# Paged values of a hybrid decoder step: eight pages and the new values of a sequence in one run of products, nine page buffers

## The chip, the cores and the metric

The kernel runs on one core of one Trainium2 chip. The metric is the device time of one execution in microseconds (us), the median of several runs. The engines are named as in the profile: PE (TensorE, with PEld for its weight loads), DVE (VectorE), ACT (ScalarE), POOL (GpSimd) and SP (SyncE, which here issues nearly all DMAs).

## The reference, cut to what matters

The program is one step of a decoder layer: a prompt of 16 + 1024 tokens, and eight sample sequences of four new tokens each, whose past keys and values lie in pages of 128 tokens. The part that the change touches is the last two lines of the sample attention:

```python
def sb_sample(q, k_new, v_new, k_past, v_past, bias):
    P, T = k_past.shape[1], q.shape[1]
    z = jnp.concatenate([sb_logits(q, k_past, bias), sb_logits(q, k_new, bias)], axis=-1)
    mask = jnp.arange(P + T)[None, :] < (P + jnp.arange(T))[:, None]
    a = stick_break_weights(z, mask)
    return (jnp.einsum('bhqk,bkhd->bqhd', a[..., :P].astype(v_past.dtype), v_past)
            + jnp.einsum('bhqk,bkhd->bqhd', a[..., P:].astype(v_new.dtype), v_new))
```

For each of 8 sequences, `v_past` is 8 pages of 128 tokens by 8 heads by 128 values in fp32 (512 KB a page), picked by a page table.

## The kernel before

The kernel is one Python program whose stages are woven together. Large projections (`inproj`, lines 336 to 353) are products of 128 x 128 weights with up to 402 columns of activations, each as three products of split numbers (lines 347 to 349). A gate (`gate_group`) is one such projection: 8 steps of 18 products, 144 in all, in four weight chunks (`wr_g` loaded by SP, `wh_g` cast by ACT, `wl_g` subtracted by DVE; two buffers of each). After each 6 products it calls `W.beat()`, so a gate has 24 beats. Side work is written as Python generators which a `Weaver` resumes at a beat; `yield 3` means "go on three beats later". What is written in this order is then placed by a scheduler, which fixes for each engine, before the run, one list of instructions. Each engine executes its list strictly in that order and waits on semaphores for its operands.

During gates 5 to 13 the paged values run as such side work:

- `chain(b)` (lines 1274 to 1297) makes the attention weights of sequence b: it loads logits `dz`, takes a softplus (`ds`, by DVE and ACT), running sums (`dc`), four products into `C` (lines 1290 to 1293), adds (lines 1294 and 1295) and an exponential into `As[b]` (`dA`, line 1297).
- `paged_values` (lines 1299 to 1336) loads pages into tiles `vr` (eight buffers) through `page_dma`, and multiplies them (`times_values`, line 1249). A page makes two products, of 32 weight columns with 512 value columns each, into 32 rows of `dO`: an even page into rows 0 to 63, an odd one into rows 64 to 127. Four products of 256 columns with the new values `vn` close a sequence (line 1332); ACT copies `dO` to `osb`, and `sample_out` transposes that into `oT`.
- The pages come in fours. While four are being multiplied, the next four are asked for, one each three beats. The first are asked for after `As[0]` exists and five more beats.

I call an **episode** a stretch in which PE runs products with 32 weight columns with no product of a gate in between. Before, a sequence has two: pages 0 to 3, and pages 4 to 7 with the new values.

Of the kernel before, what the change touches and what calls it, by code (L numbers as in the profile page):

```python
# [10 lines left out]
F32 = mybir.dt.float32  # L11
# [9 lines left out]
P = 128  # L21
# [4 lines left out]
NB = 8  # L26
# [5 lines left out]
HEADS = 8  # L32
GH = 4
DV = 256
NPG = 8
# [54 lines left out]
def hybrid_step(ctx: ExitStack, tc: tile.TileContext, x_prompt, x_sample, cache_k, cache_v, state_gla,  # L90
# [4 lines left out]
    mm = nc.tensor.matmul  # L95
    vec, act, pool = nc.vector, nc.scalar, nc.gpsimd
# [17 lines left out]
    W = Weaver()  # L114
# [80 lines left out]
    with tc.tile_pool(name="xp", bufs=2) as xp, tc.tile_pool(name="xps", bufs=5, space=PSUM) as xps:  # L195
# [109 lines left out]
        for c, (lo, hi) in enumerate(XCHUNKS):  # L305
            n = hi - lo
# [110 lines left out]
    def page_dma(dst, cache, b, i, hs):  # L417

        def load():
            return nc.sync.value_load(pt[:1, b * NPG + i:b * NPG + i + 1], min_val=0, max_val=NPOOL - 1)  # L420
        done = paged.setdefault(cache.tensor.name, [])
        if len(done) < 4:
            pg = load()
        else:
            with tc.issue_after(done[-4]):
                pg = load()
        d = nc.sync.dma_start(dst, cache[0, bass.ds(pg, 1), :, hs, :].rearrange("o p h d -> p (o h d)"))
        done.append(d.ins)
# [109 lines left out]
    with tc.tile_pool(name="sp", bufs=1) as sp, tc.tile_pool(name="sps", bufs=1, space=PSUM) as sps:  # L538
# [64 lines left out]

        def attend_tile(h, qi, qlo, qhi, j, q, kt, V, carry, O):
            nm = f"{h}_{qi}_{j}"
# [63 lines left out]
            if j == jmax:  # L669
                O[qi] = sps.tile([P, 512], F32, tag="O", name=f"O{h}_{qi}")  # L670
            if both:
                o = sps.tile([P, 512], F32, tag="O", name=f"Ob{h}")[:, :n]
                mm(o, V[0][:, j, :], ah[:, :n], start=True, stop=False, skip_group_check=True)
                mm(o, V[0][:, j, :], al[:, :n], start=False, stop=False, skip_group_check=True)
                mm(o, V[1][:, j, :], ah[:, :n], start=False, stop=True, skip_group_check=True)
                O[2] = sp.tile([P, 64], F32, tag="ob", name=f"ob{h}")
                act.copy(O[2][:], o)
                return
            o = O[qi]
            mm(o[:, col:], V[0][:nk, j, :], ah[:nk, :n], start=(j == jmax), stop=False, skip_group_check=True)  # L680
# [116 lines left out]
    with tc.tile_pool(name="gp", bufs=1) as gp, tc.tile_pool(name="gps", bufs=1, space=PSUM) as gps:  # L797
# [330 lines left out]
        for g in range(GH):  # L1128
# [26 lines left out]
            for f in range(2):  # L1155
                v = xtile(f"gv{g}_{f}")
                raws = {}
# [28 lines left out]
    with tc.tile_pool(name="dp", bufs=2) as dp, tc.tile_pool(name="dps", bufs=1, space=PSUM) as dps:  # L1186
# [15 lines left out]
        def softplus_(X, z):  # L1202
            vec.tensor_scalar(X, z, 30.0, None, ALU.min)
            act.activation(X, X, AF.Exp)
            act.activation(X, X, AF.Ln, bias=1.0)
            vec.tensor_tensor(X, z, X, ALU.max)

        def split_(src, shape, rows, tag, nm, bufs=1):
            a = dp.tile(shape, F32R, tag=tag + "h", bufs=bufs, name=f"{nm}_h")
            b = dp.tile(shape, F32R, tag=tag + "l", bufs=bufs, name=f"{nm}_l")  # L1210
            act.copy(a[:rows], src)
            vec.tensor_tensor(b[:rows], src, a[:rows].bitcast(F32), ALU.subtract)
            return a, b
# [31 lines left out]
        def times_values(O, a, v, page):  # L1245

            for f in range(2):
                j = 2 * (page % 2) + f
                mm(O[32 * j:32 * j + 32], a, v[:, f * 512:(f + 1) * 512], start=page < 2, stop=False, skip_group_check=True)

        an = dp.tile([P, NB, 32], F32, tag="an", bufs=1, name="an")
        vn = dp.tile([P, 1024], F32, tag="vn", bufs=1, name="vn")
# [19 lines left out]
        As = {}  # L1272

        def chain(b):

            while b not in z_done:
                yield 2
            z = dp.tile([P, 32, NPG], F32, tag="dz", bufs=1, name=f"dz{b}")
            nc.sync.dma_start(z[:].rearrange("p a r -> p (a r)"), zd[b][:])
            yield 6  # L1280
            vec.tensor_tensor(z[:], z[:], bias32[:].rearrange("p h t -> p (h t)").unsqueeze(2).to_broadcast([P, 32, NPG]), ALU.add)
            s = dp.tile([P, 32, NPG], F32, tag="ds", bufs=1, name=f"ds{b}")
            softplus_(s[:], z[:])
            sh, sl = split_(s[:].rearrange("p a r -> p r a"), [P, NPG, 32], P, "ds", f"ds{b}")
            sf = s[:].rearrange("p a r -> p (a r)")
            vec.tensor_tensor_scan(sf, sm8[:], sf, 0.0, ALU.mult, ALU.add)
            ch, cl = split_(s[:].rearrange("p a r -> p r a"), [P, NPG, 32], P, "dc", f"dc{b}")
            yield 8
            C = dps.tile([P, 256], F32, tag="C", name=f"C{b}")
            mm(C[:], ntri[:], sh[:].rearrange("p r a -> p (r a)"), start=True, stop=False)  # L1290
            mm(C[:], ntri[:], sl[:].rearrange("p r a -> p (r a)"), start=False, stop=False)
            mm(C[:, 32:], nones[:], ch[:, :NPG - 1].rearrange("p r a -> p (r a)"), start=False, stop=False)
            mm(C[:, 32:], nones[:], cl[:, :NPG - 1].rearrange("p r a -> p (r a)"), start=False, stop=True)
            vec.tensor_tensor(z[:], z[:], cn[:, b, :].unsqueeze(2).to_broadcast([P, 32, NPG]), ALU.add)
            vec.tensor_tensor(z[:], z[:], C[:].rearrange("p (r a) -> p a r", r=NPG), ALU.add)
            A = As[b] = dp.tile([P, NPG, 32], F32, tag="dA", bufs=2, name=f"dA{b}")
            act.activation(A[:], z[:].rearrange("p a r -> p r a"), AF.Exp)

        def paged_values():
            W.spawn(chain(0))  # L1300
            while 0 not in As:
                yield 1
            yield 5
            O = None
            pages = [(b, i) for b in range(NB) for i in range(NPG)]
            raws = {}

            def fetch(n):
                if n < len(pages):
                    b, i = pages[n]  # L1310
                    raws[n] = dp.tile([P, 1024], F32, tag="vr", bufs=8, name=f"vr{b}_{i}")
                    page_dma(raws[n][:], cache_v, b, i, slice(0, HEADS))
            for n in range(4):
                fetch(n)
            for n in range(0, len(pages), 4):
                b, i = pages[n]
                while b not in As:
                    yield 1
                if i == 0:
                    if b + 1 < NB:  # L1320
                        W.spawn(chain(b + 1))
                    O = dps.tile([P, 512], F32, tag="O", bufs=2, name=f"dO{b}")
                for e in range(4):
                    fetch(n + 4 + e)
                    yield 3
                for e in range(4):
                    times_values(O, As[b][:, NPG - 1 - i - e, :], raws.pop(n + e), i + e)
                if i == NPG - 4:

                    for j in range(4):  # L1330
                        cs = slice(j // 2 * 256, j // 2 * 256 + 256)
                        mm(O[32 * j:32 * j + 32, cs], an[:, b, :], vn[:, j % 2 * 512 + cs.start:j % 2 * 512 + cs.stop],
                           start=False, stop=True, skip_group_check=True)
                    osb = dp.tile([P, 512], F32, tag="osb", bufs=2, name=f"osb{b}")
                    act.copy(osb[:], O[:])
                    W.spawn(sample_out(b, osb), 4)

        def sample_out(b, osb):

            ps = dps.tile([P, 512], F32, tag="oT", name=f"oT{b}")  # L1340
            for h in range(4):
                nc.tensor.transpose(ps[:, h * P:(h + 1) * P], osb[:, h * P:(h + 1) * P], ident[:])
            a = ps[:]
            for f in range(2):
                own = bass.AP(tensor=a.tensor, offset=a.offset + 48 * f, ap=[list(a.ap[0]), [P + NT, 4], [1, NT], [64, 2]])
                vec.tensor_reduce(osmp[:, 4 * f:4 * f + 4, b * NT:(b + 1) * NT], own, mybir.AxisListType.X, ALU.add)
            return
            yield

        W.spawn(new_keys())  # L1350
        W.spawn(paged_values(), 8)
        for g in range(5, 14):
            gate_group(g)
# [7 lines left out]
    with ExitStack() as out:  # L1361
# [369 lines left out]
        for pair in ((1, 2), (6,), (5, 3), (7, 4)):  # L1731
            for q in range(2):
                banks = [bank(f"b{pair[0]}{q}_{t}") for t in range(4)]
                for p in pair:
                    b = {2: q, 3: 2 + q, 7: 2 + q, 4: q}.get(p)
# [45 lines left out]
```

## Time and profile before

| what | value |
|---|---|
| median of 3 runs | 2034.35 us (2033.86 to 2036.96) |
| the profiled execution | 2034.71 us, its span 2033.0 us |
| PE busy | 2004.2 us, 99% of the span |
| DVE, ACT, POOL busy | 1496.9, 1018.4, 96.1 us |
| granted PE clock, mean | 0.999 |
| stretch with value products | 1438.4 to 1649.4 us |

Busy time of PE is from modelled ends of pipelined matmuls, so that 99% does not mean that each moment carries useful work: the step from one start to the next tells more than a duration. Idle time of another engine costs nothing unless PE waits for it.

### The profile page before, as it was taken

The page shows a single profiled execution, that of the slowest core. Times are in us where ns is not written, and L with a number is a line of the kernel's source. Part 1 is how long each engine was busy: PE and PEld are TensorE (multiplying, and loading weights), DVE is VectorE, ACT ScalarE, POOL GpSimd, SP SyncE. Part 2 cuts the span into 40 slices and gives each one's busy share as a digit, 9 for nine tenths or more (in the row PEclk, how much of TensorE's full clock was granted, in tenths as well). Part 3 has the DMA queues.
Part 4 walks back from the last instruction along what each step waited for, and adds up shares of the span by engine and source line. Part 5 has one row for each costly group of instructions (what it writes and reads, how often), then busy time and mean ns, then how long its engine had stood idle before and what let it go on. Part 6 is the DMA issues. An engine that isn't in the chain of part 4 may idle for free.

```text
span 2033.0 us, 41746 instructions
## 1 busy us (share of the span) xinstructions
PE 2004.2 (99%) x12379; PEld 1852.4 (91%) x12379; DVE 1496.9 (74%) x6163; ACT 1018.4 (50%) x2377; POOL 96.1 (5%) x355
## 2 busy tenths in 40 slices
PE   6999999999999999999999999999999999999998
PEld 5999999999999999999999999999988898788776
DVE  7368888888888888899898888978444338365466
ACT  7356767675766757433535335254433335343342
POOL 0111110101000010000000000000000000000000
PEclk9999999999999999999999999999999999999999
DMA  6345554545555442433342434335767656352485
GB/s 205 98 136 161 143 163 132 175 129 157 151 161 151 141 125 77 142 101 89 103 108 80 126 79 120 90 93 176 243 220 234 221 186 221 104 176 94 141 281 204
DMA packets 371980, 301.92 MB, mean 149 GB/s; under 512 B 42336, under 2 KB 312264, under 8 KB 371752
## 3 DMA queue, kind: packets, MB, share of 16 engines
q1 hardware_dynamic: 371448, 298.73, 49.1%
q8 instruction: 97, 1.59, 0.3%
q14 instruction: 131, 1.07, 0.2%
q10 hardware_dynamic: 304, 0.53, 0.1%
HBM read 241.84 MB, written 57.31 MB: 147 GB/s over the span
## 4 chain that ended last, share of the span: by engine, by line
PE 91%; DVE 3%; DMA 2%; ACT 2%; issue 1%; SPq 0%; DVEq 0%; POOL 0%; POOLq 0%; ACTq 0%
PE acc_g L347 6%; PE acc_g L348 5%; PE acc_g L349 5%; PE b L1682 4%; PE b L1683 4%; PE b L1684 4%; PE acc_gv L347 3%; PE acc_gv L348 3%; PE acc_gv L349 3%; PE acc_k L347 3%; PE acc_k L349 3%; PE acc_k L348 3%; PE acc_q L348 3%; PE acc_q L347 3%; PE acc_q L349 3%; PE acc_v L347 3%
## 5 line engine op out<-in xcount | busy, mean ns | idle before, releaser
L470 DVE SCALAR_TENSOR_TENSOR jk<-kp,qb 128x128 f32<-128x128 f32 x2048 | 593.6, 290 | 46.2 <-DMA qb<-qsd 3.0
L347 PE MATMUL acc_g<-hT,wh_g 128*128 128x368 f32 (+2 forms) x768 | 250.7, 326 | 0.0
L348 PE MATMUL acc_g<-hT,wh_g 128*128 128x368 f32 (+2 forms) x768 | 247.2, 322 | 0.0
L349 PE MATMUL acc_g<-hT,wl_g 128*128 128x368 f32 (+2 forms) x768 | 246.9, 321 | 0.0
L470 DVE DVE_READ_ACCUMULATOR jk<-kp,qb 128x1 f32 x2048 | 167.3, 82 | 0.0
L1682 PE MATMUL b<-ring,f 128*128 128x512 f32 x416 | 163.9, 394 | 1.5 <-DVE y L1547 1.1
L1683 PE MATMUL b<-ring,f 128*128 128x512 f32 x416 | 162.3, 390 | 0.0
L1684 PE MATMUL b<-ring,f 128*128 128x512 f32 x416 | 161.9, 389 | 0.0
L347 PEld LDWEIGHTS acc_g<-hT,wh_g 128*128 128x128 f32 x768 | 144.3, 188 | 12.0 <-issue 10.7
L348 PEld LDWEIGHTS acc_g<-hT,wh_g 128*128 128x128 f32 x768 | 144.4, 188 | 0.7
L349 PEld LDWEIGHTS acc_g<-hT,wl_g 128*128 128x128 f32 x768 | 144.2, 188 | 0.0
L1481 DVE TENSOR_TENSOR ring<-wr,ring 128x512 fp32r<-128x512 f32 x104 | 71.2, 689 | 97.7 <-ACT ring L1480 97.1
L1480 ACT CAST ring<-wr 128x512 fp32r<-128x512 f32 x104 | 64.0, 620 | 134.7 <-PE b L1684 78.1
L347 PE MATMUL acc_gv<-hT,wh_gv 128*128 128x402 f32 (+2 forms) x384 | 130.1, 339 | 0.0
L347 PE MATMUL acc_k<-hT,wh_k 128*128 128x384 f32 (+1 forms) x384 | 126.1, 328 | 0.0
L348 PE MATMUL acc_gv<-hT,wh_gv 128*128 128x402 f32 (+2 forms) x384 | 125.3, 326 | 0.0
L349 PE MATMUL acc_gv<-hT,wl_gv 128*128 128x402 f32 (+2 forms) x384 | 125.0, 326 | 0.0
L349 PE MATMUL acc_k<-hT,wl_k 128*128 128x384 f32 (+1 forms) x384 | 124.7, 325 | 0.0
L348 PE MATMUL acc_k<-hT,wh_k 128*128 128x384 f32 (+1 forms) x384 | 124.4, 324 | 0.0
L347 PE MATMUL acc_q<-hT,wh_q 128*128 128x368 f32 (+2 forms) x384 | 124.3, 324 | 0.0
L348 PE MATMUL acc_q<-hT,wh_q 128*128 128x368 f32 (+2 forms) x384 | 123.6, 322 | 0.0
L349 PE MATMUL acc_q<-hT,wl_q 128*128 128x368 f32 (+2 forms) x384 | 123.3, 321 | 0.0
(483 smaller groups left out, 5263.6 us busy)
## 6 DMA issues: line engine op xcount, KB each, us to landing
kp<-in_cache_k_dram SPq DMA_DIRECT2D x512, 64.0 KB
vr<-in_cache_v_dram SPq DMA_DIRECT2D x64, 512.0 KB
qb<-qsd SPq DMA_DIRECT2D x64, 256.0 KB
wr_g<-in_w_in_dram SPq DMA_DIRECT2D x64, 256.0 KB
wr<-td SPq DMA_DIRECT2D x56, 256.0 KB
tf<-in_w_out_dram SPq DMA_DIRECT2D x48, 256.0 KB
td<-tf SPq DMA_DIRECT2D x48, 256.0 KB
wr<-in_w_out_dram SPq DMA_DIRECT2D x48, 256.0 KB
```

Of the source, the lines that this page charges most:

```text
L347: mm(acc[c][:, :n], wh, hh[k][:, lo:hi], start=(k == 0), stop=False)
L348: mm(acc[c][:, :n], wh, hl[k][:, lo:hi], start=False, stop=False)
L349: W.mark = mm(acc[c][:, :n], wl, hh[k][:, lo:hi], start=False, stop=(k == NK - 1)).ins
L470: ins = vec.scalar_tensor_tensor(jk[:], kp[:], 1.0, qbs[h, b][:, t, :], ALU.mult, ALU.mult, accum_out=zt[:, t, NPG - 1 - i:NPG - i])
L1480: act.copy(wh, r)
L1481: vec.tensor_tensor(wl, r, wh.bitcast(F32), ALU.subtract)
L1682: mm(bk[:], ah, wh, start=first and k == 0, stop=False, skip_group_check=True)
L1683: mm(bk[:], ah, wl, start=False, stop=False, skip_group_check=True)
L1684: W.mark = mm(bk[:], al, wh, start=False, stop=last and k == 7, skip_group_check=True).ins
```

## The change

`paged_values` is written anew. A sequence's eight pages and its new values are multiplied without a `yield` in between. The pages of sequence 0 are asked for at once, one each two beats, before `As[0]` exists. The pages of the next sequence are asked for after the products of this one, 3, 3, 3, 3, 3, 2, 2 and 5 beats apart, so that the last is asked for five beats ahead of the products. There are nine `vr` buffers instead of eight.

```diff
         def paged_values():
             W.spawn(chain(0))
-            while 0 not in As:
-                yield 1
-            yield 5
-            O = None
-            pages = [(b, i) for b in range(NB) for i in range(NPG)]
             raws = {}
 
-            def fetch(n):
-                if n < len(pages):
-                    b, i = pages[n]
-                    raws[n] = dp.tile([P, 1024], F32, tag="vr", bufs=8, name=f"vr{b}_{i}")
-                    page_dma(raws[n][:], cache_v, b, i, slice(0, HEADS))
-            for n in range(4):
-                fetch(n)
-            for n in range(0, len(pages), 4):
-                b, i = pages[n]
+            def fetch(b, i):
+                raws[i] = dp.tile([P, 1024], F32, tag="vr", bufs=9, name=f"vr{b}_{i}")
+                page_dma(raws[i][:], cache_v, b, i, slice(0, HEADS))
+
+            for i in range(NPG):
+                fetch(0, i)
+                yield 2
+            for b in range(NB):
                 while b not in As:
                     yield 1
-                if i == 0:
-                    if b + 1 < NB:
-                        W.spawn(chain(b + 1))
-                    O = dps.tile([P, 512], F32, tag="O", bufs=2, name=f"dO{b}")
-                for e in range(4):
-                    fetch(n + 4 + e)
-                    yield 3
-                for e in range(4):
-                    times_values(O, As[b][:, NPG - 1 - i - e, :], raws.pop(n + e), i + e)
-                if i == NPG - 4:
+                if b + 1 < NB:
+                    W.spawn(chain(b + 1))
+                O = dps.tile([P, 512], F32, tag="O", bufs=2, name=f"dO{b}")
+                for i in range(NPG):
+                    times_values(O, As[b][:, NPG - 1 - i, :], raws.pop(i), i)
 ...
+                if b + 1 < NB:
+                    for i in range(NPG):
+                        fetch(b + 1, i)
+                        yield (3, 3, 3, 3, 3, 2, 2, 5)[i]
```

What is left out are the lines of the new values, `osb` and `sample_out`, which stand one level further left and are the same.

**Place A: the list of SP as the values begin.** `dz0` are the logits of sequence 0, `vr0_0` is its page 0, `wr_g6_1` a weight chunk of gate 6. Before:

```order
L1220 DMA znall_25494<-znd_124 32x256
L1279 DMA dz0_25586<-zd0_84 128x256
L427 ISA
L427 DMA vr0_0_25795<-in_cache_v_dram 128x1024
L185 DMA wr_g6_1_25882<-in_w_in_dram 128x4x128
L1255 DMA vn_25518<-out_6_dram 32x1024
L427 ISA
L427 DMA vr0_1_25806<-in_cache_v_dram 128x1024
```

And now:

```order
L1220 DMA znall_25494<-znd_124 32x256
L427 ISA
L427 DMA vr0_0_25586<-in_cache_v_dram 128x1024
L185 DMA wr_g6_1_25981<-in_w_in_dram 128x4x128
L1255 DMA vn_25518<-out_6_dram 32x1024
L1279 DMA dz0_25597<-zd0_84 128x256
L427 ISA
L427 DMA vr0_1_25611<-in_cache_v_dram 128x1024
```

The load of `dz0` has moved behind page 0, a weight chunk and the new values.

On DVE, the list of the same place, from the first use of `dz0` on. Before:

```order
L1281 TENSOR_TENSOR dz0_25586<-dz0_25586,bias32_25474 128x256
L1224 TENSOR_TENSOR zn_25492<-zn_25492,bias32_25474 32x32
L1203 TENSOR_SCALAR ds0_25631<-dz0_25586 128x256
L1203 TENSOR_SCALAR spn_25499<-zn_25492 32x32
L1206 TENSOR_TENSOR ds0_25631<-dz0_25586,ds0_25631 128x256
L1206 TENSOR_TENSOR spn_25499<-zn_25492,spn_25499 32x32
L1236 TENSOR_TENSOR spn_25499<-spn_25499,nmask_25504 32x32
L1244 TENSOR_TENSOR spb_25515<-spn_25499,bmask_25476 32x256
L1212 TENSOR_TENSOR ds0_l_25637<-ds0_25631,ds0_h_25636 128x256
L1286 SCALAR_TENSOR_TENSOR ds0_25631<-sm8_25480,ds0_25631 128x256
L190 TENSOR_TENSOR wl_g6_0_25774<-wr_g6_0_25771,wh_g6_0_25773 128x512
L1212 TENSOR_TENSOR dc0_l_25642<-ds0_25631,dc0_h_25641 128x256
```

And now:

```order
L1244 TENSOR_TENSOR spb_25515<-spn_25499,bmask_25476 32x256
L190 TENSOR_TENSOR wl_g6_0_25898<-wr_g6_0_25895,wh_g6_0_25897 128x512
L1281 TENSOR_TENSOR dz0_25597<-dz0_25597,bias32_25474 128x256
L1203 TENSOR_SCALAR ds0_25664<-dz0_25597 128x256
L1206 TENSOR_TENSOR ds0_25664<-dz0_25597,ds0_25664 128x256
L1212 TENSOR_TENSOR ds0_l_25670<-ds0_25664,ds0_h_25669 128x256
L1294 TENSOR_TENSOR dz0_25597<-dz0_25597,cn_25522 128x256
L1286 SCALAR_TENSOR_TENSOR ds0_25664<-sm8_25480,ds0_25664 128x256
L1212 TENSOR_TENSOR dc0_l_25675<-ds0_25664,dc0_h_25674 128x256
```

The whole softplus of sequence 0 now stands behind `wl_g6_0`, the second half of the first weight chunk of gate 6, and one more addition (L1294) stands inside it.

**Place B: the list of PE at the first products with values.** `dO0` is the sum of sequence 0; rows of `acc_g` are products of a gate. Before, 90 rows further down, in the middle of gate 6:

```order
L349 MATMUL acc_g6_2_25770<-hT9_154,wl_g6_2_25964 128x304
L1249 MATMUL dO0_25839<-vr0_0_25795,dA0_25711 32x512 x2
L1249 MATMUL dO0_25839<-vr0_1_25806,dA0_25711 32x512 x2
L1249 MATMUL dO0_25839<-vr0_2_25817,dA0_25711 32x512 x2
L1249 MATMUL dO0_25839<-vr0_3_25828,dA0_25711 32x512 x2
L347 MATMUL acc_g6_0_25768<-hT10_155,wh_g6_2_25963 128x368
```

And now, at the end of gate 5:

```order
L349 MATMUL acc_g5_2_25525<-hT15_160,wl_g5_3_25738 128x304
L1249 MATMUL dO0_25845<-vr0_0_25586,dA0_25788 32x512 x2
L1249 MATMUL dO0_25845<-vr0_1_25611,dA0_25788 32x512 x2
L1249 MATMUL dO0_25845<-vr0_2_25634,dA0_25788 32x512 x2
L1249 MATMUL dO0_25845<-vr0_3_25678,dA0_25788 32x512 x2
L1249 MATMUL dO0_25845<-vr0_4_25701,dA0_25788 32x512 x2
L347 MATMUL acc_g6_0_25892<-hT0_145,wh_g6_0_25897 128x368
L348 MATMUL acc_g6_0_25892<-hT0_145,wh_g6_0_25897 128x368
L349 MATMUL acc_g6_0_25892<-hT0_145,wl_g6_0_25898 128x368
L347 MATMUL acc_g6_0_25892<-hT1_146,wh_g6_0_25897 128x368
L1249 MATMUL dO0_25845<-vr0_5_25724,dA0_25788 32x512 x2
```

The scheduler has put the products of sequence 0 90 rows sooner and broken them into four episodes: pages 0 to 4, page 5 alone, page 6 alone (17 products of the gate later), and page 7 with the new values (6 products later). The four products into `C` of sequence 0 also stand in two pairs, four products of the gate apart.

**Place C: the list of PE at a later sequence** (sequence 3; sequences 1 to 7 read alike). Before, the first of its two episodes:

```order
L349 MATMUL acc_g9_2_26855<-hT9_154,wl_g9_2_27026 128x304
L1249 MATMUL dO3_26894<-vr3_0_26701,dA3_26731 32x512 x2
L1249 MATMUL dO3_26894<-vr3_1_26739,dA3_26731 32x512 x2
L1249 MATMUL dO3_26894<-vr3_2_26774,dA3_26731 32x512 x2
L1249 MATMUL dO3_26894<-vr3_3_26831,dA3_26731 32x512 x2
L347 MATMUL acc_g9_0_26853<-hT10_155,wh_g9_2_27025 128x368
```

And now its only one, at the end of gate 8:

```order
L349 MATMUL acc_g8_2_26602<-hT15_160,wl_g8_3_26829 128x304
L1249 MATMUL dO3_26907<-vr3_0_26576,dA3_26778 32x512 x2
L1249 MATMUL dO3_26907<-vr3_1_26627,dA3_26778 32x512 x2
L1249 MATMUL dO3_26907<-vr3_2_26678,dA3_26778 32x512 x2
L1249 MATMUL dO3_26907<-vr3_3_26713,dA3_26778 32x512 x2
L1249 MATMUL dO3_26907<-vr3_4_26742,dA3_26778 32x512 x2
L1249 MATMUL dO3_26907<-vr3_5_26786,dA3_26778 32x512 x2
L1249 MATMUL dO3_26907<-vr3_6_26809,dA3_26778 32x512 x2
L1249 MATMUL dO3_26907<-vr3_7_26838,dA3_26778 32x512 x2
L1320 MATMUL dO3_26907<-vn_25518,an_25517 32x256 x4
L347 MATMUL acc_g9_0_26954<-hT0_145,wh_g9_0_26959 128x368
```

All eight pages and the new values stand in one row, once a gate of 144 products.

## Rows read from the trace of the kernel before

**Rows 1.** The page: engines (busy us), granted PE clock by slices, shares of the chain.

```profile
PE 2004.2 (99%) x12379; PEld 1852.4 (91%) x12379; DVE 1496.9 (74%) x6163; ACT 1018.4 (50%) x2377; POOL 96.1 (5%) x355
PEclk9999999999999999999999999999999999999999
PE 91%; DVE 3%; DMA 2%; ACT 2%; issue 1%; SPq 0%; DVEq 0%; POOL 0%; POOLq 0%; ACTq 0%
```

**Rows 2.** Waits of PE, whole span: us in total, times, longest; the first of nine.

```profile
PE tg L233 <- DMA grows<-in_norm_pre_g_dram: 8.1, 1, 8.1
```

**Rows 3.** Timeline of PE at sequence 0's two episodes: start us, us, instruction, count.

```profile
1438.00 0.30 PE L348 MATMUL acc_g<-hT,wh_g 128*128 128x304 f32 x1
1438.13 0.30 PE L349 MATMUL acc_g<-hT,wl_g 128*128 128x304 f32 x1
1438.36 1.92 PE L1249 MATMUL dO<-vr,dA 128*32 128x512 f32 x16
1440.22 0.43 PE L347 MATMUL acc_g<-hT,wh_g 128*128 128x368 f32 x1
1440.49 0.33 PE L348 MATMUL acc_g<-hT,wh_g 128*128 128x368 f32 x1
1440.66 0.33 PE L349 MATMUL acc_g<-hT,wl_g 128*128 128x368 f32 x1
...
1452.32 1.92 PE L1249 MATMUL dO<-vr,dA 128*32 128x512 f32 x16
1454.07 0.61 PE L1332 MATMUL dO<-vn,an 128*32 128x256 f32 x8
1454.61 0.43 PE L347 MATMUL acc_g<-hT,wh_g 128*128 128x368 f32 x1
```

**Rows 4.** Timeline of PE's weight loads in the second episode.

```profile
1452.32 0.16 PEld L1249 LDWEIGHTS dO<-vr,dA 128*32 128x32 f32 x8 [0.18 <-issue]
1452.78 0.13 PEld L1249 LDWEIGHTS dO<-vr,dA 128*32 128x32 f32 x4 [0.30 <-issue]
1453.21 0.13 PEld L1249 LDWEIGHTS dO<-vr,dA 128*32 128x32 f32 x4 [0.30 <-issue]
```

**Rows 5.** Line 1249: count, ns min/median/max, first and last start us, form.

```profile
L1249 PE MATMUL dO<-vr,dA x256: 592/592/617, 1438.4 to 1648.7; 128*32 128x512 f32 x128
```

**Rows 6.** Timeline of PE at the products into C of sequence 0.

```profile
1421.27 0.28 PE L1290 MATMUL C<-ds_h,ntri 128*128 128x256 f32 x1
...
1421.60 0.27 PE L1293 MATMUL C<-dc_l,nones 128*128 128x224 f32 x1
```

**Rows 7.** Timelines of DVE and of ACT in the chain of sequence 0.

```profile
1414.26 0.40 DVE L1281 TENSOR_TENSOR dz<-dz,bias 128x256 f32<-128x256 f32 x1
...
1418.40 0.67 DVE L190 TENSOR_TENSOR wl_g<-wr_g,wh_g 128x512 fp32r<-128x512 f32 x1
1419.27 0.62 DVE L1212 TENSOR_TENSOR dc_l<-ds,dc_h 128x256 fp32r<-128x256 f32 x1 [0.20 <-ACT dc_h L1211]
...
1422.23 0.41 DVE L1295 TENSOR_TENSOR dz<-dz,C 128x256 f32<-128x256 f32 x1
...
1416.98 0.62 ACT L187 CAST wh_g<-wr_g 128x512 fp32r<-128x512 f32 x1
...
1423.31 0.70 ACT L1297 ACTIVATE dA<-dz 128x256 f32<-128x256 f32 x1
```

**Rows 8.** Timeline of SP (DMA issues) at place A.

```profile
1411.62 0.42 SPq L1279 DMA_DIRECT2D dz<-zd  x1
1412.24 0.35 SPq L427 DMA_DIRECT2D vr<-in_cache_v_dram  x1
...
1413.96 0.33 SPq L1255 DMA_DIRECT2D vn<-out_dram  x1
```

**Rows 9.** Busy us of engines by windows, then clock, DMA share and GB/s.

```profile
1440.00:1460.00 20.00, 20.00 (x138) 17.97 (x135) 10.88 (x25) 9.68 (x21) 0.00 (x0) 1.00 0.74 236
```

**Rows 10.** Waits of SP's queue from 1400 to 1660 us: total, times, longest.

```profile
SPq L185 <- DVE wl_g L190: 76.9, 28, 7.3
```

More of the change, by code (lines that the diff above doesn't have):

```diff
@@ L1315, in paged_values @@
-            for n in range(0, len(pages), 4):
-                b, i = pages[n]
+            raws = {}
+            def fetch(b, i):
[5 more added lines that the diff above has]
+            for b in range(NB):
                 while b not in As:
                     yield 1
-                if i == 0:
-                    if b + 1 < NB:
-                        W.spawn(chain(b + 1))
-                    O = dps.tile([P, 512], F32, tag="O", bufs=2, name=f"dO{b}")
-                for e in range(4):
-                    fetch(n + 4 + e)
-                    yield 3
-                for e in range(4):
-                    times_values(O, As[b][:, NPG - 1 - i - e, :], raws.pop(n + e), i + e)
-                if i == NPG - 4:
[L1330 to L1336, printed above, removed]
@@ new lines, in paged_values @@
+                if b + 1 < NB:
[3 more added lines that the diff above has]
+                    times_values(O, As[b][:, NPG - 1 - i, :], raws.pop(i), i)
+                for j in range(4):
+                    cs = slice(j // 2 * 256, j // 2 * 256 + 256)
+                    mm(O[32 * j:32 * j + 32, cs], an[:, b, :], vn[:, j % 2 * 512 + cs.start:j % 2 * 512 + cs.stop],
+                       start=False, stop=True, skip_group_check=True)
@@ L1338, in sample_out @@
+                osb = dp.tile([P, 512], F32, tag="osb", bufs=2, name=f"osb{b}")
+                act.copy(osb[:], O[:])
+                W.spawn(sample_out(b, osb), 4)
+                if b + 1 < NB:
+                    for i in range(NPG):
+                        fetch(b + 1, i)
+                        yield (3, 3, 3, 3, 3, 2, 2, 5)[i]
         def sample_out(b, osb):
```

## The prediction

> **What bounds the kernel now.** I read the page first: PE is busy for 99% of the span and makes up 91% of the chain that ended last, and its granted clock stays at 1.00 in the slices that the change touches, the higher of its two levels, 2.4 GHz [rows 1]. Then PE's waits: there are nine in the whole span, the first of 8.1 us before the work begins [rows 2], and none of them lies between 1400 and 1700 us; PE is busy for 20.00 of the 20 us of a window there [rows 9]. So in the stretch of the values PE never waits, and the time there is the sum of the steps of PE's list from one start to the next. DVE, ACT, POOL and the transfers are covered. A change of this stretch can gain only by making PE's steps fewer or shorter, and loses whatever wait it brings to PE. Therefore I read the timeline of PE around an episode [rows 3, 4] and then the chain that feeds the first episode [rows 6 to 8].
>
> **What an episode costs.** From the last gate product before the first episode (1438.13) to the second one behind it (1440.49) pass 2.36 us. Of these, 0.13 and 0.17 are the normal steps of two gate products (1438.00 to 1438.13, 1440.49 to 1440.66), so 2.06 us belong to the 16 value instructions [rows 3]. Their weight loads come in fours, one four each 0.43 us (1452.78 to 1453.21) [rows 4]; four fours make 1.72 us. The rest, 0.34 us, is what it costs to go from products with 128 weight columns to ones with 32 and back: one part of it before the first value product, one behind the last, the first gate product standing 0.27 us before the second. The second episode fits: 1.75 us for its 16 (1452.32 to 1454.07) and 0.54 us for the new values and the way out [rows 3]. Value products are 64 pages of two, 128, and the trace has 256 instructions, so each runs as two [rows 5].
>
> **Term 1, sequences 1 to 7.** Place C shows one episode where there were two, with the same products in it. Each saves 0.34 us, seven make 2.4 us. The products themselves, the four into C, the transposes and all gate products are the same in number, and I cost them at nothing.
>
> **Term 2, sequence 0.** Place B shows four episodes where there were two: twice 0.34, +0.7 us. Further, pages 4, 5, 6 and 7 no longer stand next to a partner. An even page writes rows 0 to 63 of `dO` and an odd one rows 64 to 127, so a page uses two of the four groups of 32 columns. That loads come in fours each 0.43 us says that four instructions run side by side, one in each group; the new values, which use all four groups with half as many columns, take half that a four. A page's two instructions on one group must follow each other: two pages side by side take 0.86 us, and one page alone takes 0.86 us too. Four pages without partner take 3.44 us where they took 1.72: +1.7 us. The lower bound is 0, if a lone page's four instructions run as one four in 0.43 us; the upper is 1.7. I take 1.7, as the rows have no two instructions of one group side by side. Term 2 is +2.4 us.
>
> The Trainium skill, "TensorEngine Tiling (Array Packing)", section "Tiling Modes", says that the tiles of such a mode are independent and can load weights and multiply in parallel, and under "Theoretical Speedup" that 32 columns allow up to four times the rate. That speaks against breaking sequence 0 up: two tiles of four then stand empty. By that rule lone pages cost the 1.7 us more, and if only columns counted they would cost nothing more and the sum would be 1.7 us lower; the trace's loads in fours agree with the rule, but it has no lone page.
>
> **Term 3, the wait at C of sequence 0.** By place A, `dz0` is issued behind page 0, a weight chunk and `vn`: at about 1414.3 (1413.96 + 0.33) where it was at 1411.62 [rows 8]. Before, DVE used it at 1414.26, 2.6 us after its issue [rows 7], so now it can be there at about 1417, later by what of the page is still under way. But on DVE it also stands behind `wl_g6_0` now. Its cast on ACT began at 1416.98 and takes 0.62 us, the subtraction takes 0.67 us [rows 7]: DVE is free for `dz0` at 1418.2, and the load is then no longer what is late. That is 3.9 us later than 1414.26. From there the chain is the same (exponential, logarithm, cast, scan, cast, `dc_l`), with one addition more in it (0.4 us, as L1295) and two small steps less (about 0.2 us). `dc_l` ended at 1419.89 (1419.27 + 0.62); now at 1419.89 + 3.9 + 0.2 = 1424.0. PE reached the last product into C at 1421.60 [rows 6]; now four gate products of 0.17 stand between the two pairs, so it comes there at 1422.3 and waits 1.7 us. Nothing hides that: all that stands behind on PE's list, the rest of gate 5 first, waits too. Bounds: 0, if the softplus gets ahead as before, and 3 us, if page 0 and the weight chunk hold `dz0` up for another 1.3 us. I take 1.7, as the list of DVE is fixed.
>
> Next comes the first value product. Behind C stand an addition and the exponential `dA`, 0.41 + 0.70 us plus handovers; before, 2.14 us passed (1421.87 to 1424.01) with other work in the way [rows 6, 7]. PE has ten rows until it needs `dA`, about 1.4 us. A wait of 0 to 0.7 us; I take 0, as `dA` now follows at once on ACT. Pages: page 0 is issued at about 1411.8, page 3 behind `wr_g6_2`, which waits for `wl_g6_0` (1418.2), page 4 at about 1420. A page is 512 KB. At 236 GB/s, the rate of this stretch [rows 9], the 384 KB that it has more than `dz0` take 1.7 us, so I estimate 2.6 + 1.7 = 4.3 us from issue to landing. Page 4 lands at about 1424.3, the products begin at about 1425.5. Pages 6 and 7 are issued behind `wr_g6_3`, which waits for `wl_g6_1`, at about 1428.5 and 1429.6, and land by 1434; PE comes to them at 1433.1 and 1435.3. Page 6 is thus about even: 0 to 0.5 us, taken as 0.
>
> **The ninth buffer and the later loads.** A page of the next sequence can be loaded when PE has read the one it replaces; the ninth buffer lets one go ahead. The last page is asked for five beats ahead; a gate of 144 products at some 0.16 us is 23 us, a beat 0.96 us, so 4.8 us ahead, against a landing of 4.3 us, and PE needs page 7 only 3 x 0.86 us into the episode. But what counts is SP's list. Weight chunks wait there for `wl_g` [rows 10], which follows the end of a gate's chunk on PE, and pages stand behind them. From sequence 2 on, the chunk ahead of pages 6 and 7 waits for the first or second quarter of the gate, more than 11 us ahead of the episode: covered. Only in sequence 1 is it the third, 5.7 us ahead: cast and subtraction 1.4, the issues about 2, landing 4.3, that is 7.7 us against 5.7 + 2.6. It fits by 0.6 us; 0 to 1 us, taken as 0. Weights themselves are loaded two chunks (11 us) ahead and stay covered.
>
> **The sum.** -2.4 + 2.4 + 1.7 = +1.7 us. The profiled execution took 2034.71 us, 1.7 more than its span and 0.4 over the median of 2034.35, well inside the spread of the three runs. On the median: **2036.1 us**, 0.08% more. What a measurement of this kernel can tell from no change is about 0.2%, 4.1 us. Own range by the bounds: 1.7 lower for lone pages and 1.7 for C gives 2032.7; 1.3 + 0.7 + 0.5 + 1 higher gives 2039.6.
>
> **Rivals.** (a) The gain comes as the edit reads: sequence 0 costs no more than the others, no wait. Then eight episodes are saved, 2.7 us: 2031.6. For it: there is no wait of PE before; against it: places A and B. 20%. (b) Slower: the last pages come late in each sequence, because a page gets only five beats where the second four had twelve or more. The place is page 7 on PE's list; it decides once landing takes over 7.4 us (4.8 + 2.6) from the moment it was asked for, by SP's queue or by slower transfers. One us late in each of seven sequences is +7: 2034.35 + 1.7 + 7 = 2043.1. For it: SP's waits for `wl_g` are as long as 7.3 us [rows 10]; against it: those that stand ahead of page 7 from sequence 2 on end 11 us before. 18%. (c) Faster by more than 0.2%: all sixteen switches together cost 5.4 us and eight are the most that can go, 2.7; it takes an effect that no row shows, such as gate products that run faster. Below 2030.3. 5%.
>
> **How the numbers follow.** Forecast 57%, (a) 20%, (b) 18%, (c) 5%. Faster by over 0.2% 5%; slower by over 0.2% is (b) and the upper end of the forecast, 20%; the rest, 75%, within 0.2%. The range takes in (a) and the forecast's range, and reaches a little into (b) where one or two sequences are late: 2031.2 to 2040.6.
>
> **What would show it.** Right: value products in 11 episodes; PE waits for DVE at C of sequence 0, near 1.7 us; lone pages 0.86 us from start to gate; one stretch of about 4.2 us a sequence later on. Wrong: no wait at C (then the load and `wl_g6_0` were not what set it), lone pages of 0.43 us, waits of PE for pages in later sequences, or a lower granted clock behind a wait of PE.

## The result and the profile after

| | before | after |
|---|---|---|
| median of 22 runs each | 2034.24 us (2033.11 to 2036.96) | 2038.38 us (2036.34 to 2041.69) |
| ratio, 95% interval | | 1.0019 (1.0013 to 1.0025) |
| the profiled execution | 2034.71 us, span 2033.0 us | 2037.55 us, span 2035.6 us |

The changed kernel is 4.1 us slower (2.6 to 5.1 by the interval). That is 0.19% by the ratio and 0.20% by the medians, at the very edge of the 0.2% that the prediction counts as no change. The forecast was +1.7 us.

The page of the changed kernel reads almost like that of the kernel before [rows 1]: the same number of matmuls, PE 99% busy, the granted clock at its higher level in every slice.

```profile
PE 2006.3 (99%) x12379; PEld 1852.7 (91%) x12379; DVE 1498.9 (74%) x6163; ACT 1021.9 (50%) x2377; POOL 96.9 (5%) x355
PEclk9999999999999999999999999999999999999999
```

The difference shows only where the list of waits is cut down to the stretch of the values. Waits of PE from 1400 to 1640 us in the changed kernel (engine, line, what it waited for: us in total, times, longest); before, the same list is empty:

```profile
PE oT L1334 <- ACT osb L1323: 0.7, 1, 0.7
PE C L1292 <- ACT dc_h L1211: 0.5, 1, 0.5
PE C L1293 <- DVE dc_l L1212: 0.3, 1, 0.3
```

These make 1.5 us, and the stretch grew by 3.6. The list shows less than what a wait costs, because matmuls are pipelined and "idle" begins only when the modelled end of the last one has passed. So I added up the **steps** of PE's list instead, as the prediction did: from the start of one gate product to the start of the next, less the normal step of a gate product of its width (0.137, 0.166 or 0.173 us for 304, 368 or 384 columns, measured between neighbours). What is left over belongs to the pieces in between. From the first product of gate 5 to the first of the output projection:

| piece | before, us | after, us | difference | forecast |
|---|---|---|---|---|
| value products, sequence 0 | 4.54 | 6.89 | +2.35 | +2.4 |
| value products, sequence 1 | 4.54 | 5.09 | +0.55 | -0.34 |
| value products, sequences 2 to 7, six times | 4.54 | 4.20 | -2.04 | -2.04 |
| products into `C`, all eight sequences | 3.60 | 5.14 | +1.54 | +1.7 |
| transposes into `oT`, all eight | 3.56 | 4.74 | +1.18 | 0 |
| all that is not the normal step of a gate product | 45.00 | 48.57 | +3.57 | +1.7 |

The rows add up to 3.58. The rest of the span gave back 0.97 in these two executions (2.6 in the span against 3.57), behind the stretch, in work that the change does not touch. The medians of many runs differ by 4.1, and 3.57 lies well inside their interval.

**An episode of sequences 2 to 7** is what the edit promised. Timeline of PE in sequence 2:

```profile
1484.98 0.30 PE L349 MATMUL acc_g<-hT,wl_g 128*128 128x304 f32 x1
1485.21 3.64 PE L1249 MATMUL dO<-vr,dA 128*32 128x512 f32 x32
1488.67 0.61 PE L1320 MATMUL dO<-vn,an 128*32 128x256 f32 x8
1489.21 0.44 PE L347 MATMUL acc_g<-hT,wh_g 128*128 128x368 f32 x1
1489.49 0.33 PE L348 MATMUL acc_g<-hT,wh_g 128*128 128x368 f32 x1
```

From 1484.98 to 1489.49 are 4.51 us. Two normal steps (0.137 and 0.166) go off, and 4.20 are left: eight fours of 0.43, the new values with 0.43, and 0.33 for the switch.

**Sequence 0** is broken up as place B showed. Timeline of PE from the products into `C` on:

```profile
1421.32 0.28 PE L1290 MATMUL C<-ds_h,ntri 128*128 128x256 f32 x1
1421.52 0.39 PE L1291 MATMUL C<-ds_l,ntri 128*128 128x256 f32 x1
...
1422.27 0.34 PE L347 MATMUL acc_g<-hT,wh_g 128*128 128x384 f32 x1
1423.13 0.37 PE L1292 MATMUL C<-dc_h,nones 128*128 128x224 f32 x1 [0.53 <-ACT dc_h L1211]
1423.80 0.37 PE L1293 MATMUL C<-dc_l,nones 128*128 128x224 f32 x1 [0.29 <-DVE dc_l L1212]
...
1425.65 2.77 PE L1249 MATMUL dO<-vr,dA 128*32 128x512 f32 x20
...
1429.22 1.05 PE L1249 MATMUL dO<-vr,dA 128*32 128x512 f32 x4
1433.22 1.05 PE L1249 MATMUL dO<-vr,dA 128*32 128x512 f32 x4
```

L1292 could start at 1422.44, one step behind the gate product at 1422.27; it starts 0.69 us later. L1293 could follow within some 0.1 us, as in [rows 6], and comes 0.56 us later than that. These are 1.25 us (the list names 0.8), and the split of the four products into two pairs costs the rest. The five pages 0 to 4 take 2.90, the lone page 5 takes 1.19 and the lone page 6 1.18, which is 0.33 for the switch and 0.86 for the page, as forecast.

**Sequence 1** got its page 7 late. Timeline of SP there (the last row, from a narrower window, is page 7, the second of the two that the row above it takes together):

```profile
1451.96 0.39 SPq L185 DMA_DIRECT2D wr_g<-in_w_in_dram  x1
1453.46 1.49 SPq L427 DMA_DIRECT2D vr<-in_cache_v_dram  x2
...
1454.62 0.33 SPq L427 DMA_DIRECT2D vr<-in_cache_v_dram  x1
```

And of PE:

```profile
1456.34 4.10 PE L1249 MATMUL dO<-vr,dA 128*32 128x512 f32 x30
1459.83 0.62 PE L1320 MATMUL dO<-vn,an 128*32 128x256 f32 x4
1460.27 0.60 PE L1249 MATMUL dO<-vr,dA 128*32 128x512 f32 x2
1460.69 0.60 PE L1320 MATMUL dO<-vn,an 128*32 128x256 f32 x4
1461.23 0.43 PE L347 MATMUL acc_g<-hT,wh_g 128*128 128x368 f32 x1
```

Page 7 is issued at 1454.62, 1.7 us before the episode, and its products begin at 1459.8, 5.2 us later. In sequence 2 the new values begin 3.46 us into the episode, here 3.49, and half of page 7 comes behind them. The view of line 1249 puts it on the load:

```profile
  DMA vr<-in_cache_v_dram: 0.8, 1
```

**The transposes** are what the prediction had not priced. Timeline of PE in sequence 6:

```profile
1601.50 0.44 PE L347 MATMUL acc_g<-hT,wh_g 128*128 128x368 f32 x1
...
1606.31 0.66 PE L1334 MATMUL oT<-ident,osb 128*128 128x128 f32 x4 [0.69 <-ACT osb L1323]
```

And of ACT, up to its copy of `dO`:

```profile
1599.26 0.67 ACT L1211 CAST dc_h<-ds 128x256 fp32r<-128x256 f32 x1 [1.43 <-DVE ds L1286]
1599.84 0.46 ACT L532 COPY gx<-acc_g 128x368 f32<-128x368 f32 x1
...
1605.26 0.52 ACT L520 ACTIVATE gs<-gs 128x384 f32<-128x384 f32 x1 [0.87 <-DVE gs L519]
1605.69 0.57 ACT L1323 COPY osb<-dO 128x512 f32<-128x512 f32 x1
```

The episode ends at 1601.50, but ACT copies `dO` only at 1605.69, 4.2 us later. ACT takes its list in order, and ahead of the copy stand the casts of the next sequence's chain, and behind these what a gate's end brings: copies out of the accumulators (`gx`) and the exponentials of the gate, one of which itself waits 0.87 us for DVE. PE, whose list has four beats between episode and transposes, reaches them 4.0 us behind the episode and arrives first. Before, the copy began 0.8 us behind the end of the episode of sequence 0, which is at 1454.61 [rows 3]:

```profile
1455.39 0.57 ACT L1335 COPY osb<-dO 128x512 f32<-128x512 f32 x1
```

A gate's end alone does not make the copy late: in sequence 1 the episode also stands at a gate's end, and the copy follows 0.1 us behind it. In sequences 3 to 6 it goes by the load `dz`, from which the next chain starts. Timeline of SP and of DVE in sequence 6:

```profile
1588.48 0.34 SPq L427 DMA_DIRECT2D vr<-in_cache_v_dram  x1
1589.38 0.33 SPq L1279 DMA_DIRECT2D dz<-zd  x1
1595.01 0.43 DVE L1281 TENSOR_TENSOR dz<-dz,bias 128x256 f32<-128x256 f32 x1 [6.40 <-DMA dz<-zd]
```

DVE stood idle 6.40 us for `dz7`, which was used 5.6 us after its issue, and the copy begins 10.7 us after that use. In sequences 3, 4 and 5 the copy also begins 10.7 to 10.8 us after the use of the next `dz`; it stands 3.6, 3.0 and 3.2 us behind the episode there. It takes 0.57 us, so it is done just in time in 4 and 5, and too late in 3 and 6 (by the steps 0.3 and 0.9 us). `dz4` to `dz7` took 4.4 to 5.6 us from issue to use here, each issued 0.9 to 1.2 us behind a page; in the kernel before, where the last page was 4 to 5 us ahead, they took 2.8 to 3.2. With 2.9 us for `dz7` the copy would stand some 1.5 to 2 us behind the episode (1.5 by the 10.7 us; sequence 2, whose next `dz` was used 3.0 us ahead of the episode's end, has 1.8) and PE would not wait; that is an estimate from these numbers.

### The profile page after: what moved, and what is told of

Read it like the earlier page. It is cut to its first block, busy times and chain, and to the rows that moved or that the text cites. A ratio compares the mean times of both kernels' runs of the same rounds, so it can differ in the third digit from the quotient of the medians.

```text
span 2035.6 us, 41729 instructions
## 1 busy us (share of the span) xinstructions
PE 2006.3 (99%) x12379; PEld 1852.7 (91%) x12379; DVE 1498.9 (74%) x6163; ACT 1021.9 (50%) x2377; POOL 96.9 (5%) x355
## 4 chain that ended last, share of the span: by engine, by line
PE 88%; DVE 5%; DMA 3%; ACT 2%; issue 1%; SPq 0%; DVEq 0%; POOL 0%; POOLq 0%; ACTq 0%
PE acc_g L347 5%; PE acc_g L348 5%; PE acc_g L349 5%; PE b L1674 5%; PE b L1675 4%; PE b L1676 4%; PE acc_gv L347 3%; PE acc_gv L348 3%; PE acc_gv L349 3%; PE acc_k L347 3%; PE acc_k L349 3%; PE acc_k L348 3%; PE acc_q L348 3%; PE acc_q L347 3%; PE acc_q L349 3%; PE acc_v L347 3%
## 5 line engine op out<-in xcount | busy, mean ns | idle before, releaser
L347 PE MATMUL acc_g<-hT,wh_g 128*128 128x384 f32 (+2 forms) x768 | 250.0, 326 | 0.0
L348 PE MATMUL acc_g<-hT,wh_g 128*128 128x384 f32 (+2 forms) x768 | 247.3, 322 | 0.0
L349 PE MATMUL acc_g<-hT,wl_g 128*128 128x384 f32 (+2 forms) x768 | 246.9, 321 | 0.0
```

Source lines behind the costliest of these rows:

```text
L347: mm(acc[c][:, :n], wh, hh[k][:, lo:hi], start=(k == 0), stop=False)
L348: mm(acc[c][:, :n], wh, hl[k][:, lo:hi], start=False, stop=False)
L349: W.mark = mm(acc[c][:, :n], wl, hh[k][:, lo:hi], start=False, stop=(k == NK - 1)).ins
```

## The experiments

Each kernel is compared with the kernel before on the same chip; medians of before there were 2035.9 us (first four) and 2035.6 us (last three). "Stage" is the sum of the table above that is not the normal step of gate products, against the 45.00 of the kernel before.

| kernel | ratio, 95% interval | stage against before |
|---|---|---|
| e1_late_first | 0.9990 (0.9981 to 0.9999) | -2.66 us |
| e2_transposes_later | 1.0014 (1.0005 to 1.0023) | +2.82 |
| e3_four_sooner | 1.0029 (1.0018 to 1.0040) | +3.95 |
| e4_pages_0213 | 0.9995 (0.9986 to 1.0004) | +0.21 |
| e5_two_page_episodes | 1.0025 (1.0016 to 1.0035) | +4.84 |
| e6_single_pages | one run, 2078.36 us | +39.3 |
| e7_z_before_pages | 1.0004 (0.9995 to 1.0013) | +0.80 |

**Theory**: joining the episodes gains 0.34 us for each one saved; the loss comes from asking for sequence 0's pages early, which breaks its episode and puts `dz0` behind them, and from the place of the later episodes, where the copy `osb` comes late. **Rivals**: the joined episodes give no gain, because the last pages come late (rival (b)); or early pages hurt by their traffic alone.

### The joined episodes without the early pages

The changed kernel; sequence 0's pages wait for `As[0]` as they did before.

```diff
+            while 0 not in As:
+                yield 1
             for i in range(NPG):
                 fetch(0, i)
                 yield 2
```

> The changed kernel with one part undone: the pages of sequence 0 are asked for only once its weights As[0] exist, as before; one episode a sequence and nine buffers stay. Theory (the loss is at the first sequence, from pages asked for ahead of dz0, and the joined episodes gain what was forecast): no wait at C of sequence 0, sequence 0 in one episode, eight switches of 0.34 us fewer than in the kernel before, so -2.7 us: about 2031.5 us, ratio 0.9987. Rival (joined episodes cost in later sequences too, by late pages and by osb late on ACT): PE waits in sequences 1 to 7, and a time at or above that of before, 2034 to 2036 us.

Measured: 2033.9 us, ratio 0.9990, about 2 us less than before, and -2.66 us by the steps, where eight saved switches of 0.34 make 2.7. PE has no wait between 1400 and 1640 us. Timeline of PE in sequence 0:

```profile
1436.86 0.34 PE L349 MATMUL acc_g<-hT,wl_g 128*128 128x384 f32 x1
1437.13 3.64 PE L1249 MATMUL dO<-vr,dA 128*32 128x512 f32 x32
1440.58 0.61 PE L1322 MATMUL dO<-vn,an 128*32 128x256 f32 x8
1441.13 0.41 PE L347 MATMUL acc_g<-hT,wh_g 128*128 128x304 f32 x1
```

All eight sequences take 4.21 us. So the joining works and gives what was worked out for it; what the changed kernel lost comes with the early pages and the shifted places, which this run takes back together. This kernel has the lowest ratio of all that ran; its interval ends below 1, though by a hair. It changes more than the early pages: its episodes stand 84 products into a gate, and `dz3` to `dz7`, with no page issued shortly ahead of them, are used 2.8 to 2.9 us after their issue. The copy `osb` then follows 0.1 us behind each of these episodes.

### The transposes later

The changed kernel; the transposes stand eight beats behind the episode in place of four.

```diff
-                W.spawn(sample_out(b, osb), 4)
+                W.spawn(sample_out(b, osb), 8)
```

> The changed kernel with sample_out called eight beats behind an episode instead of four, so that the transposes into oT stand 48 gate products behind it instead of 24. Theory (PE waits there for the copy osb on ACT, 1.2 us in the profile in sequences 3 and 6): these waits go, about 1.2 us less than the changed kernel: 2037.2 us, ratio 1.0014 to before. Rival (the waits are of that one execution): no difference, 2038.4 us.

Measured: 1.0014. The interval includes the changed kernel's 1.0019, so the time alone doesn't settle it; the steps do. The wait for `osb` is gone from PE's list, which keeps the two at `C` (0.5 and 0.3 us, the same rows as above), and the eight transposes take 3.6 us in place of 4.74. In sequence 6 PE comes to them with no wait:

```profile
1609.13 0.60 PE L1334 MATMUL oT<-ident,osb 128*128 128x128 f32 x4
```

ACT copies `osb` at 1604.76 here, 3.5 us behind the episode's end (4.2 in the changed kernel), behind the same rows of ACT. That the waits go has two parts, which this run does not separate: PE comes four beats later, and `dz7` came 0.7 us sooner (used 4.9 us after its issue), so that the copy did too, again 10.7 us after the use of `dz7`. Some 0.4 us of the gain were lost again at `C` of sequence 1, where the last of the four products now waits for its input (0.83 us in place of 0.45).

### Early pages without joining

The kernel before; its first pages are asked for at once, and everything else stays.

```diff
-            while 0 not in As:
-                yield 1
-            yield 5
             O = None
```

> The kernel before with only its start changed: the first four pages of sequence 0 are asked for at once, the two episodes a sequence stay. Theory (asking for pages ahead of dz0 delays the chain, whatever the episodes look like): PE waits 1 to 2.5 us at C of sequence 0, 2035.2 to 2036.7 us. Rival (the early pages are harmless, only the joining costs): as before, 2034.2 us.

Measured: 1.0029, about 6 us (3.7 to 8.1), more than expected. Value products take 36.24 us (36.32 before), so it isn't the pages. The products into `C` take 6.95 in place of 3.60. Timeline of PE at `C` of sequences 0 and 1:

```profile
1428.46 0.39 PE L1290 MATMUL C<-ds_h,ntri 128*128 128x256 f32 x1
1429.16 0.39 PE L1291 MATMUL C<-ds_l,ntri 128*128 128x256 f32 x1
1430.95 0.37 PE L1292 MATMUL C<-dc_h,nones 128*128 128x224 f32 x1 [0.22 <-ACT dc_h L1211]
1431.70 0.37 PE L1293 MATMUL C<-dc_l,nones 128*128 128x224 f32 x1
...
1441.25 0.37 PE L1292 MATMUL C<-dc_h,nones 128*128 128x224 f32 x1 [0.91 <-ACT dc_h L1211]
1441.92 0.37 PE L1293 MATMUL C<-dc_l,nones 128*128 128x224 f32 x1 [0.30 <-DVE dc_l L1212]
```

`dz0` is issued at 1419.59, 8.0 us later than before [rows 8]. In sequence 0 the four products stand in four places, the first 7.2 us later than before [rows 6], and cost 1.87 us where four together cost 0.45. In sequence 1 they stand in two pairs with a wait between: 2.38 in place of 0.45. I had expected the wait of sequence 0 alone. So page requests in front of `dz` make the products into `C` costly even when no episode is joined. It is only in part the wait that the prediction's term names: the list of waits has 0.2 us in sequence 0, and much of the rest there is that the four products stand alone. How much of it is waiting this run does not show.

### dz0 ahead of the pages

The changed kernel with a pause of three beats ahead of sequence 0's first page, so that SP issues `dz0` first (at 1412.50, page 0 at 1413.12).

```diff
+            yield 3
             for i in range(NPG):
                 fetch(0, i)
                 yield 2
```

> The changed kernel, with a pause of three beats ahead of the first page of sequence 0, so that the load of dz0 stands in front of the pages on SP's list again, while the pages still come sooner than in the kernel before. PE's list then has the four products into C together, and sequence 0 in four episodes (pages 0123, 45, 6, 7 and the new values); the other sequences keep one episode, eighteen gate products into a gate. Theory: no wait at C of sequence 0 (-1.5 us against the changed kernel), sequence 0 in 2.05 + 1.19 + 1.19 + 1.62 = 6.05 us (-0.8), no wait of the transposes for osb (-1.2), page 7 of sequence 1 late by 0 to 0.9: against the kernel before -2.4 + 1.5 + 0 to 0.9, so 0.9996 to 1.0000. Rival (pages sooner hurt by themselves, by the traffic that they put beside the weights, wherever dz0 stands): the wait at C stays, 1.0010 or more.

Measured: 1.0004. The products into `C` of sequence 0 stand together again and wait for nothing:

```profile
1422.14 0.28 PE L1290 MATMUL C<-ds_h,ntri 128*128 128x256 f32 x1
...
1422.48 0.27 PE L1293 MATMUL C<-dc_l,nones 128*128 128x224 f32 x1
...
1433.26 1.05 PE L1249 MATMUL dO<-vr,dA 128*32 128x512 f32 x4 [0.95 <-DMA vr<-in_cache_v_dram]
```

The transposes take 3.6 us and sequence 1 4.21, both without a wait. Sequence 0 took 7.07 us, not 6.05: the last row is its page 6, which came 1.0 us late. It was issued at 1428.00, behind a weight chunk at 1426.29, and its products began 5.3 us later. By the steps the sum is +0.80: -0.9 was expected with page 7 of sequence 1 in time, as it is here; the late page adds 1.0, `C` of sequence 1 adds 0.4 (its four products stand together, but the last waits for `dc_l`), and 0.3 lies in small pieces. So the wait at `C` of sequence 0 comes from what stands ahead of `dz0`, not from the traffic of early pages; that they are early gains nothing either. With `dz0` first on SP's list, its softplus also stands ahead of `wl_g6_0` on DVE again (DVE takes `dz0` at 1415.13). The run does not separate these two lists.

### More episodes

The kernel before with a beat in the middle of each four of pages.

```diff
                 for e in range(4):
+                    if e == 2:
+                        yield 1
                     times_values(O, As[b][:, NPG - 1 - i - e, :], raws.pop(n + e), i + e)
```

> The kernel before, with one beat (six gate products) between the second and the third page of each four. The pages stay in pairs, C and the transposes stay where they are; the value products stand in 29 episodes in place of 16. Theory (each episode costs 0.34 us beyond its products): 13 x 0.34 = +4.4 us, about 2038.6 us, ratio 1.0022. Rival (the 0.34 us is not a cost of each change of product form, but belongs to the first episode behind other work): no difference, 1.0000. By the theory the first two pairs of sequence 0 show 0.34 + 0.86 = 1.20 us each between normal gate steps.

Measured: 1.0025, about 5 us. Value products take 40.79 us in place of 36.32: 4.47 for 13 more episodes, 0.344 each. Timeline of PE at one pair of pages:

```profile
1437.24 0.30 PE L349 MATMUL acc_g<-hT,wl_g 128*128 128x304 f32 x1
1437.47 1.06 PE L1249 MATMUL dO<-vr,dA 128*32 128x512 f32 x8
1438.47 0.44 PE L347 MATMUL acc_g<-hT,wh_g 128*128 128x368 f32 x1
1438.74 0.33 PE L348 MATMUL acc_g<-hT,wh_g 128*128 128x368 f32 x1
```

From 1437.24 to 1438.74 are 1.50 us, less 0.137 and 0.166: 1.20, as expected. The Trainium skill, "TensorEngine Tiling (Array Packing)", section "Key Properties" under "Tiling Modes", says that a change of the tiling mode drains the engine. The trace agrees, with 0.34 us for the way in and out together.

### Single pages

The kernel before with a beat between any two pages.

```diff
                 for e in range(4):
+                    if e:
+                        yield 1
                     times_values(O, As[b][:, NPG - 1 - i - e, :], raws.pop(n + e), i + e)
```

> The kernel before, with a beat between any two pages, so that nearly every page stands alone: 59 episodes in place of 16, and 56 pages without a partner beside them. Theory (a switch 0.34 us, a lone page 0.86 us where a partnered one is worth 0.43): 43 x 0.34 + 56 x 0.43 = 14.6 + 24.1 = +38.7 us, about 2073. Rival (only the columns count, so a lone page costs 0.43 us, and it was the waiting for pages that made lone pages long in the changed kernel): +14.6 us, about 2049. One look, read from the steps of PE's list.

Measured: 2078.36 us in a single run, 43 us over before; by the steps +39.3, where 38.7 were expected. A lone page with its switch, on PE's timeline:

```profile
1440.34 0.30 PE L349 MATMUL acc_g<-hT,wl_g 128*128 128x304 f32 x1
1440.57 1.05 PE L1249 MATMUL dO<-vr,dA 128*32 128x512 f32 x4
1441.55 0.44 PE L347 MATMUL acc_g<-hT,wh_g 128*128 128x368 f32 x1
1441.83 0.33 PE L348 MATMUL acc_g<-hT,wh_g 128*128 128x368 f32 x1
```

1441.83 less 1440.34 and two normal steps is 1.19 us, of which 0.34 are the switch: one page alone takes 0.85, as long as two side by side (the row of 8 above). The lower bound of the prediction's term 2 (a lone page in 0.43 us) is out.

### Pages in another order

The kernel before with the pages of a four in the order 0, 2, 1, 3, so that two pages which use the same half of the columns stand next to each other.

```diff
-                for e in range(4):
+                for e in (0, 2, 1, 3):
                     times_values(O, As[b][:, NPG - 1 - i - e, :], raws.pop(n + e), i + e)
```

> The kernel before with each four pages multiplied in the order 0, 2, 1, 3, so that two pages that use the same 64 columns stand next to each other. It measures whether PE starts value products strictly in the order of its list. If it does, page 1 waits behind page 2, which waits for page 0: a four takes 2.57 us instead of 1.72, 16 of them +13.7 us, 2048 us. If products of free column groups go ahead of ones that wait, as the new values seemed to beside the lone page 7: no difference, 2034.2 us.

Measured: 0.9995, no difference. An episode of 16 takes 1.94 us where it took 1.92 [rows 3]:

```profile
1439.32 1.94 PE L1249 MATMUL dO<-vr,dA 128*32 128x512 f32 x16
```

A product whose group of columns is free starts although one ahead of it in the list waits for its own group: strict order would have made an episode of 16 some 0.85 us longer. So the sentence in the section on the kernel before, that each engine executes its list strictly in order, is not true of PE's products with 32 weight columns. What costs is a page that has no partner in its episode at all, not the order inside an episode.

## Why the prediction was right, and where its size was off

The time is inside the range, and the change is the slight loss that was forecast, but the sum was 1.7 where 3.57 (steps) and 4.1 (medians) were measured. That the change still counts as none by the prediction's 0.2% is partly luck: 4.1 us lie on that line, and about half of them are two terms that the sum has at 0. By its own steps:

- **What bounds the kernel**: right. PE's steps account for the whole difference of the stretch, and by the steps no single wait of PE in it passed 0.9 us.
- **Term 1, 0.34 us for each joined episode**: right. 0.34 in six of seven sequences, 0.344 over 13 added episodes (e5), and 2.66 for eight where nothing else got in the way (e1).
- **Term 2, sequence 0 broken into four**: right, +2.35 against +2.4. Lone pages cost 0.86, at the upper bound that was taken; e6 shows it some fifty times over.
- **Term 3, the wait at `C`**: right in place and cause, and nearly so in size, +1.54 against 1.7. The 1.7 were waiting alone; measured are 1.25 of waiting and 0.3 for the split into two pairs, which the prediction did not price. `dz0` was issued at 1414.42 (forecast 1414.3), DVE took it at 1417.95, straight behind `wl_g6_0` (1418.2), and `dc_l` ended at 1423.74 (1424.0). e7 puts `dz0` first, and the wait goes. `dA` and page 6 were taken as 0, and PE waited for neither.
- **The later loads, sequence 1**: mis-sized. The prediction found a margin of 0.6 us and took 0; it was short by 0.89. Of those 1.5 us, 0.6 lie on SP's list (page 7 issued 1.7 us ahead of the episode; the working has 5.7 less 3.4, or 2.3) and 0.9 in the landing: 5.2 us from issue to use, where 4.3 were estimated from one load of 128 KB and a mean rate. e7's page 6 took 5.3. From sequence 2 on, no page was late, as forecast, so rival (b) has its mechanism but only in the sequence that the prediction had singled out.
- **The transposes**: the missed term, +1.18. "The products themselves, the four into C, the transposes and all gate products are the same in number, and I cost them at nothing": the number is the same, but they stand elsewhere, and their input `osb` comes later. The step that was missing is a look at `dz` of the later sequences. The prediction saw for sequence 0 that a page ahead of `dz` makes the chain late, and did not ask it again for `dz4` to `dz7`, which now stand 0.9 to 1.2 us behind a page and are used 4.4 to 5.6 us after their issue. The late chain stands ahead of the gate's end and of `osb` in ACT's list. That the copy begins 10.7 to 10.8 us after the use of `dz` in four sequences here, and in four of e2, shows this path. That it is the page just ahead which makes `dz` slow is argued from comparison, and no run varies it alone: with a page 0.9 to 1.2 us ahead, e2 has 3.7 to 4.9 us and e3 4.3 to 4.6 (`dz4` to `dz6`); with the last page some 4 us ahead, e7 has 2.1 to 2.2.

The two missed terms make 2.07 us, and with them the sum is 3.8, which is near the steps (3.57) and the medians (4.1). Rival (a) was wrong for this kernel but is what e1 does: with sequence 0 in one episode and no wait, 0.9990.

Left open: why e6's run lies 3 us above what its steps say (a single run), and which part of e3's +5.9 us lies outside the stretch (the steps give 3.95, the interval reaches down to 3.7). All waits and steps are read from one execution of each kernel. No run joins the episodes with eight buffers, so what the ninth is worth is not shown.

## What to carry to other kernels

Where PE is the bound, count what an edit makes of PE's list piece by piece: each change of product form (0.34 us here) and each page without a partner (0.43) had the same price wherever it stood, and both can be counted in the list before the kernel has run. An edit that moves work along that list also moves it against the lists of the other engines: for each consumer on PE, look at what its producer's engine has queued ahead at the new place, and which load that waits for. And a request that is made earlier, or closer to another, goes ahead of something: ask at every place, not only at the first, what now stands behind it in the queue.

## What the runs showed of the hardware

- Products of 32 weight columns start past a waiting one: in e4 the order 0, 2, 1, 3 costs nothing (1.94 us for 16 against 1.92), and in the changed kernel the first half of the new values (1459.83) starts ahead of the second half of a late page 7 (1460.27), though it stands behind it in the list.
- A wait of PE costs more than the list of waits shows: at `C` of sequence 0 the list has 0.8 us, and the two products start 1.25 us later than they could.
- A page of 512 KB took 5.2 and 5.3 us from issue to first use in two places where PE stood waiting for it, at some 220 GB/s on the whole (the mean from 1400 to 1640 us of the changed kernel is 222).
- A load of 128 KB (`dz4` to `dz7`) took 2.1 to 2.2 us from issue to use in e7 and 2.8 to 3.2 before, with the last page of 512 KB issued some 4 us ahead or more, and 4.4 to 5.6 us in the changed kernel and 3.7 to 4.9 in e2, with a page 0.9 to 1.2 us ahead. That the page ahead is the reason is not shown by a run of its own.
